# Second attention of an encoder trunk: packed 32-row score matmuls, and one written order for three engines

## The chip, the cores and the metric

One NeuronCore of a Trainium2 chip runs the whole program. The metric is device time in microseconds (us) for one execution, lower is better. Matrices are multiplied by TensorE (PE), sums, maxima and subtractions run on VectorE (DVE), exponentials and copies on ScalarE (ACT), more elementwise work on GpSimd (POOL), and SyncE (SP) issues most transfers (DMAs). SBUF is the working memory with 128 partitions (rows); matmuls write to PSUM, eight banks of 128 x 512 numbers.

## The reference

Two layers over 1024 tokens of 1024 features. The change lies in the attention of the second one (multi-head latent attention, 16 heads), whose core is:

```python
q = (rmsnorm(cq, q_norm) @ w_uq).reshape(B, S, N_HEADS_B, 64 + 32)
q_nope, q_rope = q[..., :64], q[..., 64:]
kv = (rmsnorm(ckv, kv_norm) @ w_ukv).reshape(B, S, N_HEADS_B, 64 + 64)
k_nope, v = kv[..., :64], kv[..., 64:]
q_rope, k_rope = rope(q_rope, cos, sin), rope(k_rope, cos, sin)
s = einsum(q_nope, k_nope) + einsum(q_rope, k_rope)      # k_rope is shared by the heads
p = softmax(s * scale)
o = einsum(p, v)
y = (o * silu(gate)) @ w_out
```

So a score sums 64 products of the head's own part and 32 of the rotary part.

## The kernel before, in words

Products are made accurate with a split: a number x is a rounded high part h (type float32r) and a low part l = x - h. A product a*b is then three matmuls, a_h b_h + a_h b_l + a_l b_h; `mm3` (lines 90 to 94) issues them.

The program is one instruction stream per engine, built by Python loops. `run` (line 109) puts the parts into `manual_schedule(engines=FIXED)`, where FIXED is PE and SP: those two engines issue in the order in which the Python code is written. The order of ACT, DVE and POOL is chosen by the framework's scheduler.

`layer_b_in` (line 1015) makes the latents of the second layer. `latents_t` (line 1083) transposes them, and puts the shared rotary key into rows 64 to 127 of the key tiles `kb`, high and low, with zeros between, for even and odd heads at different rows. `b_rope_rows` (line 1224) copies those rows by DMA from POOL's queue to the key tile of a later head; three pairs of key tiles serve the heads in turn. The last step of `layer_b_in` weaves the last two gate products with the first pair's `b_turn` and `b_qk` (line 1159).

`b_turn` (line 1238) makes the rotary queries for four heads: a product into PSUM, multiplications by cosines and sines on DVE, sums of 32 rows on POOL. `b_qk` (line 1265) makes the queries and keys of a pair of heads: for each half of the tokens a product for q (six matmuls) and one for k (three), whose high parts ACT copies and whose low parts DVE subtracts, head by head on 64 rows; ACT and POOL put the rotary rows beside them. `b_v` (line 1206) makes the values of four heads in four products. `b_weights` (line 1189) splits the next pair's weights, and `b_wload` (line 1175) loads those behind.

`layer_b_attention` (line 1316) sweeps 128 units u: one head and 128 queries against all 1024 keys, eight units a head, 16 a pair. For each u:

- `front` (line 1321): the scores s, two halves of 512 keys with three matmuls of 128 rows each, into one of two PSUM tiles of two banks.
- `soft` (line 1333): DVE takes the negative maximum of a row (line 1336).
- `expo` (line 1339): ACT takes the exponential with its sum (line 1344); every fourth unit DVE takes reciprocals of four sums (line 1348).
- `middle` (line 1367), for u - 2: PE transposes the eight blocks of the probabilities (line 1376) into two of four rotating PSUM banks (tag "t"); ACT copies the high part (line 1379), DVE subtracts the low part (line 1380).
- `back` (line 1384), for every two units: 16 matmuls of 256 queries give the output (line 1396) in one bank; ACT copies both halves of its rows (lines 1405, 1406), POOL adds them and multiplies by the gate (lines 1407, 1408). Every second time the reciprocal sums are transposed (line 1399) and `spread` (line 1350) sends them through DRAM to all rows; `normalise` (line 1361) multiplies them in on POOL.

Projections for later heads are Python generators, of which the loop (lines 1413 to 1454) runs one step here and there between the units. In the last pair the loop loads and splits output weights and splits the first outputs (`b_yt`, line 1465). `layer_b_out` (line 1500) does the output product and the normalisation.

PSUM in this stage: two tiles of two banks for scores, four banks for everything else. SBUF tiles of 4 KB a row come from two pools, G with 33 and H with 14.

## Time and profile before

| | us |
|---|---|
| median of 3 runs | 1358.07 |
| lowest, highest | 1356.69, 1358.98 |
| the profiled execution | 1356.85 |
| its span, first to last instruction | 1355.1 |
| first score matmul, first output matmul in it | 776.2, 1246.6 |

The span is what the profile shows; the profiled execution's own time is 1.75 us longer. A row of a group names the line of the kernel, the engine, the operation, what is written and read, the count, and behind the bar the busy time in us and the mean length of one in ns. A matmul's record lasts longer than the distance to the next one's start, because matmuls are pipelined; how long a stretch takes is read from starts. A row of waits names who waited, for whom, the total in us, the count and the longest. In a row of stretches the busy times of PE, its weight loads (PEld), DVE, ACT and POOL stand with their counts, then the granted clock of TensorE, the DMA share and GB/s. Rows of SPq are issues of DMAs.

### The profile page before, as it was taken

The page shows a single profiled execution, that of the slowest core. Times are in us where ns is not written, and L with a number is a line of the kernel's source. Part 1 is how long each engine was busy: PE and PEld are TensorE (multiplying, and loading weights), DVE is VectorE, ACT ScalarE, POOL GpSimd, SP SyncE. Part 2 cuts the span into 40 slices and gives each one's busy share as a digit, 9 for nine tenths or more (in the row PEclk, how much of TensorE's full clock was granted, in tenths as well). Part 3 has the DMA queues.
Part 4 walks back from the last instruction along what each step waited for, and adds up shares of the span by engine and source line. Part 5 has one row for each costly group of instructions (what it writes and reads, how often), then busy time and mean ns, then how long its engine had stood idle before and what let it go on. Part 6 is the DMA issues. An engine that isn't in the chain of part 4 may idle for free.

```text
span 1355.1 us, 20458 instructions
## 1 busy us (share of the span) xinstructions
PE 1328.6 (98%) x7435; PEld 1143.5 (84%) x7435; DVE 855.9 (63%) x1480; ACT 799.1 (59%) x1631; POOL 565.3 (42%) x552
## 2 busy tenths in 40 slices
PE   9999999999999999999999999999999999999997
PEld 7888888888888888888988888898889889898776
DVE  7645445445544345376733378878787788777887
ACT  4665556544444423165632397889698878887411
POOL 0333123213231477425533444734654473444861
PEclk8999999999999999999999999999999999999999
DMA  9423211113244374371163011111121111113322
GB/s 369 146 35 64 33 58 54 49 27 126 96 132 132 92 179 160 124 252 47 50 182 115 2 33 34 24 38 25 32 52 28 30 25 28 25 55 124 110 93 93
DMA packets 45117, 114.30 MB, mean 84 GB/s; under 512 B 6893, under 2 KB 13342, under 8 KB 45017
## 3 DMA queue, kind: packets, MB, share of 16 engines
q1 hardware_dynamic: 40204, 100.41, 24.0%
q0 software_dynamic: 4192, 12.27, 3.7%
q8 instruction: 59, 0.97, 0.3%
q14 instruction: 42, 0.34, 0.1%
q10 hardware_dynamic: 620, 0.31, 0.1%
HBM read 96.43 MB, written 8.67 MB: 78 GB/s over the span
## 4 chain that ended last, share of the span: by engine, by line
PE 78%; DVE 7%; ACT 7%; DMA 3%; issue 3%; SPq 0%; ACTq 0%; DVEq 0%
PE pj L92 8%; PE pj L94 8%; PE pj L93 8%; PE o L1396 6%; PE t L1376 5%; PE po L92 4%; PE po L93 4%; PE po L94 4%; PE s L92 3%; PE s L94 3%; PE s L93 3%; PE pg L92 2%; PE pg L93 2%; PE pg L94 2%; PE ip L272 2%
## 5 line engine op out<-in xcount | busy, mean ns | idle before, releaser
L92 PE MATMUL pj<-uh,wh 128*128 128x512 f32 x528 | 217.2, 411 | 0.7 <-ACT wh L104 0.7
L94 PE MATMUL pj<-uh,wl 128*128 128x512 f32 x528 | 207.0, 392 | 0.0
L93 PE MATMUL pj<-ul,wh 128*128 128x512 f32 x528 | 206.8, 392 | 0.0
L1336 DVE TENSOR_REDUCE mb<-s 128x1 f32<-128x1024 f32 x128 | 155.8, 1217 | 48.7 <-PE s L94 47.9
L1380 DVE TENSOR_TENSOR ptl<-t,pth 128x512 fp32r<-128x512 f32 x256 | 165.3, 681 | 5.2 <-ACT pth L1379 3.0
L1379 ACT CAST pth<-t 128x512 fp32r<-128x512 f32 x256 | 139.5, 590 | 37.4 <-PE t L1376 34.0
L1344 ACT ACTIVATE pr<-s,mb 128x1024 f32<-128x1024 f32 x128 | 144.2, 1126 | 15.4 <-DVE mb L1336 14.7
L105 POOL TENSOR_TENSOR wl<-wraw,wh 128x1024 fp32r<-128x1024 f32 x42 | 106.3, 2536 | 102.4 <-ACT wh L104 75.4
L1376 PEld LDWEIGHTS t<-ident,pr 128*128 128x128 f32 x1024 | 119.3, 141 | 19.1 <-DVE ptl L1380 2.8
L1376 PE MATMUL t<-ident,pr 128*128 128x128 f32 x1024 | 133.1, 273 | 2.1 <-DVE ptl L1380 2.1
L1396 PE MATMUL o<-pth,vq 128*128 128x256 f32 x512 | 130.4, 292 | 1.1 <-DVE ptl L1380 1.1
L1396 PE MATMUL o<-ptl,vq 128*128 128x256 f32 x512 | 125.6, 283 | 0.8 <-DVE ptl L1380 0.5
L564 ACT ACTIVATE sb<-sb,stat 128x256 f32<-128x256 f32 (+1 forms) x144 | 67.0, 466 | 94.8 <-DVE stat L558 94.7
L94 PEld LDWEIGHTS pj<-uh,wl 128*128 128x128 f32 x528 | 99.1, 188 | 22.2
L1407 POOL TENSOR_TENSOR osum<-osum 64x256 f32<-64x256 f32 x64 | 47.9, 748 | 163.7 <-ACT osum L1406 162.6
L92 PEld LDWEIGHTS pj<-uh,wh 128*128 128x128 f32 x528 | 99.7, 189 | 15.1 <-ACT wh L104 1.1
L93 PEld LDWEIGHTS pj<-ul,wh 128*128 128x128 f32 x528 | 99.8, 189 | 14.0
L92 PE MATMUL s<-kb,q 128*128 128x512 f32 x256 | 105.8, 413 | 0.1
L94 PE MATMUL s<-kb,q 128*128 128x512 f32 x256 | 100.4, 392 | 0.0
L93 PE MATMUL s<-kb,q 128*128 128x512 f32 x256 | 100.4, 392 | 0.0
L1396 PEld LDWEIGHTS o<-ptl,vq 128*128 128x128 f32 x512 | 97.8, 191 | 1.7 <-DVE ptl L1380 1.7
L1396 PEld LDWEIGHTS o<-pth,vq 128*128 128x128 f32 x512 | 97.6, 191 | 1.8 <-DVE ptl L1380 1.7
(289 smaller groups left out, 3128.2 us busy)
## 6 DMA issues: line engine op xcount, KB each, us to landing
wraw<-wa SPq DMA_DIRECT2D x36, 512.0 KB
ada<-ada_row SPq DMA_DIRECT2D x64, 256.0 KB
wraw<-wo_a SPq DMA_DIRECT2D x18, 512.0 KB
ada<-ada_ss SPq DMA_DIRECT2D x16, 512.0 KB
kb<-kb POOLq DMA_DIRECT2D x30, 256.0 KB, 4.5
f<-f_d SPq DMA_DIRECT2D x18, 256.0 KB
xr<-x SPq DMA_DIRECT2D x8, 512.0 KB
xn_d<-z POOLq DMA_DIRECT2D x8, 512.0 KB, 4.5
```

The source lines that it names most:

```text
L92: mm(out, wh, xh, start=start, stop=False)
L93: mm(out, wh, xl, start=False, stop=False)
L94: mm(out, wl, xh, start=False, stop=stop)
L105: (lo_engine or self.nc.gpsimd).tensor_tensor(l[:, :width], raw[:, :width], f32(h[:, :width]), op=ALU.subtract)
L564: nc.scalar.activation(sb[:, a * w : a * w + w], sb[:, a * w : a * w + w], AF.Exp, bias=stat[:, 0, hh, t : t + 1], scale=-1.0, accum_out=s ...
L1336: nc.vector.tensor_reduce(m[:, 0:1], s, axis=AX.X, op=ALU.max, negate=True)
L1344: nc.scalar.activation(pr, s, AF.Exp, bias=m[:, 0:1], accum_out=dens[u // 8][:, u % 8 : u % 8 + 1])
L1376: nc.tensor.transpose(pt[:, c * P : c * P + P], pr[:, kt * P : kt * P + P], self.ident)
L1379: nc.scalar.copy(h, src)
L1380: nc.vector.tensor_tensor(l, src, f32(h), op=ALU.subtract)
L1396: nc.tensor.matmul(po[:, 0:256], v, pts[j][x][:, c * 256 : c * 256 + 256], start=n == 0, stop=n == 15)
L1407: nc.gpsimd.tensor_tensor(w3[mine, 0:256], w3[mine, 256:512], w3[mine, 0:256], op=ALU.add)
```

## The change

The work is done in cycles w of two units (the same head, 256 queries), and three things change.

**Scores.** A score has 64 x 3 + 32 x 3 = 288 rows of products where the old form used three matmuls of 128. The new one uses two full matmuls and 32 rows of a third. In the first, queries `qa` hold the high part in rows 0 to 63 and the low part in 64 to 127, against the key's high part in both. In the second, `qb` holds the high part above and the rotary rows, high and low, below, against the key's low part and the rotary key's low and high part. What is left, high rotary query times high rotary key, has 32 rows: `small` issues it for two units and two halves of the keys as four matmuls at `tile_position` rows 0, 32, 64 and 96, from a query tile `q3` whose four row groups hold the two units' queries, and a key tile `kr` that holds the two halves of the keys. They end the sums of the first unit and begin those of the second.

**Placing.** High and low parts of q and k are now split for both heads in one instruction of 128 rows (`staged`), and SP's queue carries the 64-row pieces to their places. The rotary queries go to DRAM (`b_rope_store`) and from there to `qb` and `q3` (`b_rotary`). The rotary key rows stay in the three key tiles for all heads.

**Order.** The stage runs under ORDERED: ACT and DVE also issue as written. One cycle's order is the loop below; a cycle has the rest of a projection at one place, mostly one projection a cycle (four in the first, two in some that make values). Of the output, ACT copies one half of the rows and DVE adds the other from PSUM.

The core of the diff, where `high`, `low`, `turned`, `maximum`, `expo` and `values` hold the same instructions as `middle`, `soft`, `expo` and `back` did, for one unit a (0 or 1) of a cycle or for both:

```diff
+ORDERED = FIXED | {mybir.EngineType.Activation, mybir.EngineType.DVE}
...
-                    self.layer_b_attention()
+                    with tc.manual_schedule(engines=ORDERED):
+                        self.layer_b_attention()
...
+        self.kr = self.M.tile([P, 512], F32R, name="kr")
...
-            for e, (h, l) in enumerate(self.kb):
-                dst.append((h[64:128, c : c + P], l[64:128, c : c + P], slice(64 - 64 * e, 128 - 64 * e), 3))
...
+            for rows in ((slice(0, P),) if i < 4 else (slice(32, 64), slice(96, 128))):
+                nc.scalar.copy(self.kr[rows, sl], pt[rows, 3 * P : 4 * P])
+            nc.vector.tensor_tensor(
+                self.kb[0][1][64:96, c : c + P], pt[32:64, 3 * P : 4 * P], f32(self.kr[32:64, sl]), op=ALU.subtract
+            )
...
+                weave((first, 5184.0), (self.b_turn_first(), 2600.0))
...
-        weave((chain(gate(6, 1, self.mbank), gate(7, 1, self.mbank)), 10368.0), (chain(self.b_turn(0), self.b_qk(0)), 9000.0))
+        weave((chain(gate(6, 1, self.mbank), gate(7, 1, self.mbank)), 10368.0), (self.b_qk_first(), 4500.0))
...
-    def b_rope_rows(self, hd):
-
-        for src, dst in zip(self.kb[(hd - 2) % 3], self.kb[hd % 3]):
-            self.nc.gpsimd.dma_start(dst[64:128, :], src[64:128, :])
+    def b_rope_rows(self):
+        dma, first = self.nc.gpsimd.dma_start, self.kb[0][1]
+        for j in range(2):
+            dma(first[96:128, j * 512 : j * 512 + 512], self.kr[32 * j : 32 * j + 32, :])
+        for n in (1, 2):
+            dma(self.kb[n][1][64:128, :], first[64:128, :])
...
+    def b_rope_store(self, rd, ab, sl, engine):
         nc = self.nc
+        hl = self.ht(F32R, "rope")
+        nc.scalar.activation(hl[:, 0:512], ab[:, 0:512], AF.Copy)
+        engine.tensor_tensor(hl[:, 512:1024], ab[:, 0:512], f32(hl[:, 0:512]), op=ALU.subtract)
+        for a in range(2):
+            for x in range(2):
+                nc.sync.dma_start(rd[:, x, a, :, sl], f32(hl[64 * a : 64 * a + 64, x * 512 : x * 512 + 512]))
...
+    def b_turn(self, p, hf):
+        nc = self.nc
+        if hf == 0:
+            self.b_rope_rows_d(p)
+        sl = slice(hf * 512, hf * 512 + 512)
+        ps = self.b_product(self.wu[p], 384, sl)
+        ab = []
+        def turn():
+            t = self.ht(F32, "ab")
+            for i in range(2):
+                nc.vector.tensor_tensor(t[:, i * 512 : i * 512 + 512], ps, self.tabs[i][:, sl], op=ALU.mult)
+            if hf:
+                self.tabs = None
+            w = self.ht(F32, "absw")
+            for a in range(2):
+                nc.sync.dma_start(w[64 * a : 64 * a + 64, 0:512], t[64 - 64 * a : 128 - 64 * a, 512:1024])
+            for rows, op in ((slice(0, 64), ALU.subtract), (slice(64, 128), ALU.add)):
+                nc.gpsimd.tensor_tensor(t[rows, 0:512], t[rows, 0:512], w[rows, 0:512], op=op)
+            ab.append(t)
+        def store():
+            self.b_rope_store(self.rope_d[p], ab.pop(), sl, nc.gpsimd)
+        return turn, store
...
+    def b_rotary(self, p):
+        nc = self.nc
+        third = (self.ht if p else self.gt)(F32R, "q3")
+        rd = self.rope_d.pop(p)
+        for e, (qa, qb, k) in enumerate(self.heads):
+            rows = rd[2 * (p % 2) + e]
+            nc.sync.dma_start(f32(qb[64:128, :]), rows.rearrange("x a c t -> (x a c) t"))
+            q3 = third[:, e * 512 : e * 512 + 512]
+            for g in range(4):
+                src = rows[0].rearrange("a c (i z t) -> (a c) i z t", z=2, t=P)[:, :, g // 2, :]
+                nc.sync.dma_start(f32(q3[32 * g : 32 * g + 32, :]).rearrange("p (i t) -> p i t", t=P), src)
+            self.q[2 * p + e] = (qa, qb, q3)
+    def b_qk(self, p, kind, hf):
...
+        heads = self.heads
+        up, down = slice(0, 64), slice(64, 128)
+        if kind == "q":
+            ps = self.b_product(w, 0, sl)
+            places = [(((qa, up), (qb, up)), ((qa, down),)) for qa, qb, k in heads]
+        else:
+            ps = self.mbank()
+            ch, cl = self.lat[2]
+            self.mm3(ps, h[:, 256:384], l[:, 256:384], ch[:, sl], cl[:, sl], True, True)
+            places = [(((k[0], up), (k[0], down)), ((k[1], up),)) for qa, qb, k in heads]
+        def staged():
+            hl = self.ht(F32R, "hl")
+            nc.scalar.copy(hl[:, 0:512], ps)
+            nc.vector.tensor_tensor(hl[:, 512:1024], ps, f32(hl[:, 0:512]), op=ALU.subtract)
+            for x in range(2):
+                for e in range(2):
+                    src = f32(hl[64 * e : 64 * e + 64, x * 512 : x * 512 + 512])
+                    for t, rows in places[e][x]:
+                        nc.sync.dma_start(f32(t[rows, sl]), src)
...
+        def full(w, a):
+            hd, t = w // 4, 2 * (w % 4)
+            (qa, qb, q3), k = self.q[hd], self.kb[hd % 3]
+            ts = slice((t + a) * P, (t + a) * P + P)
+            for n, (q, kk) in enumerate(((qa, k[0]), (qb, k[1]))):
+                for j in range(2):
+                    ks = slice(j * 512, j * 512 + 512)
+                    nc.tensor.matmul(sc[w][a][:, ks], q[:, ts], kk[:, ks], start=n == a == 0, stop=n == a == 1)
+            if a and w % 4 == 3:
+                self.q.pop(hd)
+        def small(w):
+            hd, t = w // 4, w % 4
+            q3 = self.q[hd][2]
+            for g in range(4):
+                rows = slice(32 * g, 32 * g + 32)
+                ks = slice((g % 2) * 512, (g % 2) * 512 + 512)
+                nc.tensor.matmul(
+                    sc[w][g // 2][:, ks], q3[rows, t * P : t * P + P], self.kr[rows, :],
+                    start=g >= 2, stop=g < 2, tile_position=(32 * g, 0),
+                )
...
+        def output(w):
+            hd, t0 = w // 4, (w % 4) * 256
+            e, po = hd % 2, ob.pop(w)
+            mine, other = slice(64 * e, 64 * e + 64), slice(64 - 64 * e, 128 - 64 * e)
+            g = self.gT[hd // 2][mine, t0 : t0 + 256]
+            w3 = self.ht(F32, "osum")
+            nc.scalar.copy(w3[mine, 0:256], po[other, 0:256])
+            if w % 2:
+                spread(w // 2, po)
+            nc.vector.tensor_tensor(w3[mine, 256:512], po[mine, 0:256], w3[mine, 0:256], op=ALU.add)
+            nc.gpsimd.tensor_tensor(g, w3[mine, 256:512], g, op=ALU.mult)
...
+        for w in range(nw + 2):
+            p, r = divmod(w, 8)
+            now, old = w < nw, 1 <= w <= nw
+            more = p + 1 < NPAIR_B
+            if now:
+                sc[w] = [self.PB.tile([P, 1024], F32, tag="s", bufs=2, name=self.nm("s")) for _ in range(2)]
+                full(w, 0)
+                small(w)
+            if old:
+                turned(w - 1, 0)
+            if now:
+                maximum(w, 0)
+            if old:
+                high(w - 1, 0)
+                low(w - 1, 0)
+                if w % 2 == 0:
+                    reciprocal(w - 1)
+            if now:
+                expo(w, 0)
+                full(w, 1)
+                maximum(w, 1)
+            if old:
+                turned(w - 1, 1)
+                high(w - 1, 1)
+                low(w - 1, 1)
+            splits = []
+            if p % 2 == 0 and now and r < 2:
+                splits += [self.b_v(p // 2, j) for j in (range(4) if w == 0 else () if w == 1 else (2 * r, 2 * r + 1))]
+            if more and r == 3:
+                self.b_heads(p + 1)
+            if more and 3 <= r <= 6:
+                splits.append(self.b_qk(p + 1, "kqkq"[r - 3], (r - 3) // 2))
+            if more and p % 2 and r in (0, 2):
+                turn, store = self.b_turn(p + 1, r // 2)
+                splits.append(turn)
+                rot.append((w + 1, store))
+            late = splits.pop() if w >= 8 and r == 1 and p % 2 == 0 and splits else None
+            for f in splits[:2]:
+                f()
+            if now:
+                expo(w, 1)
+            for f in splits[2:]:
+                f()
+            if more and r == 6:
+                self.b_rotary(p + 1)
+            if w >= 2:
+                values(w - 2)
+                output(w - 2)
+            if late:
+                late()
+            while rot and rot[0][0] <= w:
+                rot.pop(0)[1]()
+            if w == 0:
+                self.b_weights(1)
+            if r == 7 and p + 2 < NPAIR_B:
+                self.b_weights(p + 2)
+                if p % 2 == 0:
+                    self.b_tabs()
+            if p == 7:
+                if r < 4:
+                    self.b_wo_load(r)
+                if 1 <= r <= 4:
+                    self.b_wo_split(r - 1, nc.gpsimd)
+                if r >= 5:
+                    self.b_yt(r - 5, 0)
+                if r == 7:
+                    for b in range(4, 8):
                         self.b_wo_load(b)
+            if w == nw:
+                self.b_yt(3, 0)
                 self.b_rows()
                 self.b_out_blocks(0, range(4))
+            if w == nw + 1:
                 self.b_out_blocks(1, range(4))
+            if w >= 5 and w % 2:
+                normalise((w - 5) // 2)
```

More of the change, by code (lines that the diff above doesn't have):

```diff
@@ L1133, in layer_b_in @@
                 gq[b + 2] = self.bw_load(b + 2)
-            for _ in gate(b, 0, self.bank if b < 2 else self.mbank):
-                pass
+            first = gate(b, 0, self.bank if b < 2 else self.mbank)
+            if b < 7:
+                for _ in first:
+                    pass
+            else:
+                weave((first, 5184.0), (self.b_turn_first(), 2600.0))
             if b == 0:
@@ L1147, in layer_b_in @@
                 self.kb.append([self.ht(F32R, "kb") for _ in range(2)])
-                self.b_rope_rows(2)
+                self.b_rope_rows()
             if b == 1:
@@ new lines, in staged, with direct @@
+        def staged():
[7 more added lines that the diff above has]
+                        nc.sync.dma_start(f32(t[rows, sl]), src)
+        def direct():
+            for e in range(2):
+                src = ps[64 * e : 64 * e + 64, :]
+                for t, rows in places[e][0]:
+                    nc.scalar.copy(t[rows, sl], src)
+            for e in range(2):
+                (t, rows), = places[e][1]
+                h, hr = places[e][0][0]
+                nc.vector.tensor_tensor(t[rows, sl], ps[64 * e : 64 * e + 64, :], f32(h[hr, sl]), op=ALU.subtract)
@@ L1313, in mbank, with b_qk_first @@
+        return staged if p else direct
+    def b_qk_first(self):
+        self.b_heads(0)
+        self.b_rotary(0)
+        for hf in range(2):
+            for kind, cost in (("q", 1300.0), ("k", 650.0)):
+                split = self.b_qk(0, kind, hf)
+                yield cost
+                split()
+                yield 0.0
     def mbank(self, name="m"):
@@ new lines, in turned, with part, high @@
+        def turned(w, a):
+            pr = prs.pop((w, a))
+            tb[w, a] = []
+            for j in range(2):
+                t = self.mbank("t")
+                for c in range(4):
+                    kt = 4 * j + c
+                    nc.tensor.transpose(t[:, c * P : c * P + P], pr[:, kt * P : kt * P + P], self.ident)
+                tb[w, a].append(t)
+        def part(w, a, j, x):
+            return pts[w][j][x].rearrange("p (k q) -> p k q", k=4)[:, :, a * P : a * P + P]
+        def high(w, a):
+            if a == 0:
+                pts[w] = [(self.gt(F32R, "pth"), self.gt(F32R, "ptl")) for _ in range(2)]
+            for j in range(2):
+                nc.scalar.copy(part(w, a, j, 0), tb[w, a][j].rearrange("p (k q) -> p k q", k=4))
@@ new lines, in low, with values @@
+        def low(w, a):
+            for j, t in enumerate(tb.pop((w, a))):
+                src = t.rearrange("p (k q) -> p k q", k=4)
+                nc.vector.tensor_tensor(part(w, a, j, 1), src, f32(part(w, a, j, 0)), op=ALU.subtract)
+        def values(w):
+            hd = w // 4
+            po = ob[w] = self.mbank("o")
+            x = [(kt, x) for kt in range(8) for x in range(2)]
+            for n, (kt, i) in enumerate(x):
+                v = self.vq[hd // 4][kt // 2][:, (kt % 2) * 512 + (hd % 4) * P : (kt % 2) * 512 + (hd % 4) * P + P]
+                c = (kt % 4) * 256
+                nc.tensor.matmul(po[:, 0:256], v, pts[w][kt // 4][i][:, c : c + 256], start=n == 0, stop=n == 15)
+            pts.pop(w)
+            if w % 16 == 15:
+                self.vq.pop(hd // 4)
+            if w % 2:
+                nc.tensor.transpose(po[0:4, 256:384], dens[hd][:, 2 * (w % 4) - 2 : 2 * (w % 4) + 2], self.ident)
```

248 lines of the change are left out of this document (69 added, 179 removed).

## The prediction

> **What bounds the kernel now.** I read the page's busy times first, then the busy times by stretch of the second attention, then who waited for whom in it, then TensorE's timeline over one cycle (two units of 128 queries).
>
> ```profile
> span 1355.1 us, 20458 instructions
> PE 1328.6 (98%) x7435; PEld 1143.5 (84%) x7435; DVE 855.9 (63%) x1480; ACT 799.1 (59%) x1631; POOL 565.3 (42%) x552
> ```
> ```profile
> core 0: us, PE busy (x) PEld busy (x) DVE busy (x) ACT busy (x) POOL busy (x), PEclk, DMA share, GB/s
> 911.40:972.20 60.80, 60.31 (x394) 53.63 (x393) 48.49 (x66) 48.26 (x96) 30.16 (x33) 1.00 0.13 30
> 972.20:1033.00 60.80, 59.56 (x398) 53.14 (x397) 48.68 (x68) 52.94 (x106) 31.74 (x36) 1.00 0.15 35
> ```
> ```profile
> PE m L92 <- DVE kb L1306: 3.3, 7, 0.5
> PE t L1376 <- DVE ptl L1380: 2.1, 3, 0.8
> PE o L1396 <- DVE ptl L1380: 1.1, 2, 0.8
> ```
>
> A pair of heads (eight cycles) takes 60.8 us and TensorE is busy for about 60 of them; VectorE and ScalarE for 48 to 53. TensorE's waits in the whole second attention are the three rows of the last fence, 6.5 us together. So the stage is TensorE's own instruction stream, at a full granted clock, and what counts is how much of it goes. Busy time overlaps, so lengths must be read from starts:
>
> ```profile
> 1002.99 0.40 PE L92 MATMUL s<-kb,q 128*128 128x512 f32 x1
> 1003.22 0.40 PE L93 MATMUL s<-kb,q 128*128 128x512 f32 x1
> ...
> 1004.15 0.40 PE L94 MATMUL s<-kb,q 128*128 128x512 f32 x1
> 1004.38 1.03 PE L1376 MATMUL t<-ident,pr 128*128 128x128 f32 x8
> 1005.17 0.47 PE L92 MATMUL s<-kb,q 128*128 128x512 f32 x1
> 1005.49 0.39 PE L93 MATMUL s<-kb,q 128*128 128x512 f32 x1
> ...
> 1006.64 1.04 PE L1376 MATMUL t<-ident,pr 128*128 128x128 f32 x8
> 1007.43 0.36 PE L1396 MATMUL o<-pth,vq 128*128 128x256 f32 x1
> ...
> 1009.42 0.27 PE L1399 MATMUL o<-ident,den 128*4 128x128 f32 x1
> 1009.45 0.48 PE L92 MATMUL s<-kb,q 128*128 128x512 f32 x1
> ```
>
> One cycle without a projection lasts from 1002.99 to 1009.45, 6.46 us. Six score matmuls fill 1004.38 - 1002.99 = 1.39 us, 0.232 each; eight transposes 0.79; the values 1.99. The first matmul behind transposes is followed after 0.32 instead of 0.23: changing back from a transpose costs 0.09, changing to one nothing.
>
> **The term that matters: score matmuls.** There are twelve of 512 columns a cycle now. The change keeps eight and adds one packed group of four, each on 32 rows, into four different banks. So 4 x 0.232 = 0.93 us a cycle go, and X, the length of the packed group, comes. Projections, values and transposes keep their matmuls and cancel out. No row shows a packed group. From below, X is one matmul's 0.23, if four go side by side and the change of mode is free. From above it is four in turn with a change on both sides, 0.93 + 2 x 0.09 = 1.11. The nearest rows for "fewer rows, then all rows" stand at the start, at a slow clock:
>
> ```profile
> 7.55 1.02 PE L348 MATMUL pl<-oh,rb 33*128 33x512 f32 x2
> 8.50 1.18 PE L165 MATMUL pz<-zeros 128*128 128x512 f32 x2
> 9.47 0.85 PE L220 MATMUL pm<-sc,ada 128*128 128x1 f32 x4
> ```
>
> Two matmuls on 33 rows take 0.95, the two full ones behind them 0.97: no extra is seen at that border, which speaks for the lower half, though these rows aren't placed in tiles. I take X = 0.23 for the stream, + 3 x 0.05 because each further tile needs its own weights (a transpose, a load of 128 columns and a pass of 128, takes 0.79 / 8 = 0.10, half of it the load), + 0.09 for one change back = 0.47. A cycle gains 0.93 - 0.47 = 0.46, and 64 cycles 29 us. At the ends of X it is 45 us gained or 12 us lost.
>
> The Trainium skill (TensorE: Matmul & The Clock Gate, Measured speedup vs the span model) gives 3.07 times for four K=32 row tiles at N=512. By it X would be 0.93 / 3.07 = 0.30 and the gain about 40 us; no run here shows it yet.
>
> **Can the other engines follow a cycle of 6.0 us?** ScalarE and VectorE get a written order too, so a late step holds all that is queued behind it. These are their slots:
>
> ```profile
> 1004.58 1.23 DVE L1336 TENSOR_REDUCE mb<-s 128x1 f32<-128x1024 f32 x1
> 1005.72 1.28 DVE L1380 TENSOR_TENSOR ptl<-t,pth 128x512 fp32r<-128x512 f32 x2
> 1006.92 1.22 DVE L1336 TENSOR_REDUCE mb<-s 128x1 f32<-128x1024 f32 x1
> ```
> ```profile
> 1002.18 1.12 ACT L1344 ACTIVATE pr<-s,mb 128x1024 f32<-128x1024 f32 x1
> ...
> 1003.28 0.59 ACT L1379 CAST pth<-t 128x512 fp32r<-128x512 f32 x1
> ...
> 1005.02 1.07 ACT L1379 CAST pth<-t 128x512 fp32r<-128x512 f32 x2 [0.38 <-PE t L1376]
> 1005.98 1.13 ACT L1344 ACTIVATE pr<-s,mb 128x1024 f32<-128x1024 f32 x1
> ```
>
> A maximum holds VectorE for 1.14 us, a pair of low parts 1.20; an exponential holds ScalarE 1.10, a pair of casts 0.96. Count from the first packed matmul of a cycle. TensorE: packed group to 0.47, transposes to 1.26, second unit's full rows to 2.28, transposes to 3.07, values to 5.06, next first unit's full rows to 6.0. A matmul's record is 0.39 long where the next starts after 0.23, so a result is there 0.16 behind its slot. VectorE: first maximum 0.63 to 1.8, low parts to 3.0, second maximum to 4.1, low parts to 5.3. ScalarE: casts from 1.1 to 2.1, exponential to 3.2, casts to 4.2, second exponential to 5.3. The next packed group writes the bank that this exponential reads, at 6.0: 0.7 us in hand, less what the semaphores take. The sum of the two halves of the output moves from GpSimd to VectorE:
>
> ```profile
> L1279 DVE TENSOR_TENSOR q<-m,q 64x512 fp32r<-64x512 f32 x32 | 22.0, 688 | 27.6 <-ACT q L1278 27.1
> L1405 ACT COPY osum<-o 64x256 f32<-64x256 f32 x64 | 23.5, 368 | 3.3 <-PE o L1396 1.7
> L1407 POOL TENSOR_TENSOR osum<-osum 64x256 f32<-64x256 f32 x64 | 47.9, 748 | 163.7 <-ACT osum L1406 162.6
> L1471 DVE TENSOR_TENSOR ytb<-gT,ytb 128x512 fp32r<-128x512 f32 x11 | 16.4, 1497 | 6.1 <-ACT ytb L1470 6.1
> ```
>
> Half of L1279's columns make it some 0.35 to 0.4 us, from about 5.8 (behind ScalarE's copy) to 6.2; the next maximum is due at 6.63. VectorE's 5.2 us of work in a plain cycle fit in 6.0 with 0.4 in hand. I cost the move at nothing; without that cover it is 0.4 x 64 = 26 us. ScalarE sheds a copy of 0.37. A cycle with a query projection adds 6 x 0.23 = 1.39 to TensorE and at most 0.69 to VectorE, so there the cover grows. The banks rotate by four: the second of two projections in a cycle (the values' projections) makes the probabilities' product wait from 4.5 for a low part that ends at 4.7; 0.2 us in six cycles, 1 us. A rotary step's cast stands at the end of ScalarE's next cycle, 12.7 counted from its own cycle's group: multiplies to 6.7, two swaps through SP by 8.8 (prices below), two sums on GpSimd of 1.5 (L1407's 0.75 for half as many columns) by 11.8. I cost it at nothing; were GpSimd 2 us late, ScalarE's casts and TensorE's transposes behind them would lose 1 us, six times.
>
> **Transfers.** The split halves of q and k now go through SP's queue: six pieces a projection, 24 a pair, and ten rotary pieces a pair. What they would cost is seen on SP:
>
> ```profile
> 797.91 0.27 SPq L1358 DMA_DIRECT2D den_d<-rden  x1
> 799.08 0.45 SPq L1359 DMA_DIRECT2D rden<-den_d  x1
> ```
>
> An issue of 64 rows takes 0.45 us, and a write is followed by its reader after 1.2. In the seventh cycle of a pair 6 + 10 issues stand in line, 7.2 us from about 5.3 on. The first head's eleven are out by 10.3 and landed by 11.5; the next pair's first score is due at 7.4 + 6.0 - 0.9 = 12.5. So one microsecond in hand; behind these SP holds the denominators' round trip, which GpSimd needs a cycle later. I take 2 us for all seven joints; with the cover gone it is 1 to 2 us each, up to 14. GpSimd loses the key rows' copies and half of the output's sum; busy for 30 to 32 us of a pair now, it stays far from a bound.
>
> **Ends.** Cycle 1 has no values to hide its chain: 1.5 us. The first pair's rotary rows now go through DRAM before the first score: four multiplies of 0.69, two sums and a split of up to 1.5, a cast of 0.6, four writes and the first head's five reads of 0.45, and two landings of 1.2 make 14.3 us, against the 66 matmuls of gate and projections at 0.23, 15.2, behind the last rotary product. VectorE has the projections' splits beside it: 0 to 3 us lost, I take 1. In the last pair three steps like L1471, 1.5 us each, enter VectorE's order with 0.4 in hand: 3 x 1.1 less what the next cycles return, 2. The 3.3 us at L1306 go, since that wait was for a bank whose reader is now placed ahead. With the joints and the banks, 1.5 + 1 + 2 + 2 + 1 - 3.3 = 4 us are lost.
>
> **Sum.** The profiled execution took 1356.85 us, 1.75 more than its span; 29 - 4 = 25 us less gives 1332. The median of the three runs, 1358.07, is 1.2 above the profiled one, so I put 1333.
>
> **Rivals.**
> *The array must be empty at each change.* A matmul is 0.39 long at a spacing of 0.23, so 0.16 is still in flight; if the group waits for that and the transposes wait for the group, X = 0.23 + 0.15 + 2 x 0.16 = 0.70, the gain 15 - 4 = 11 us, the time 1347. Against it: the border at L348 shows nothing. The Trainium skill (TensorEngine Tiling (Array Packing), Key Properties) says that a change of tiling mode drains TensorE, which is this rival; the trace has no change of that kind. Chance 0.15.
> *The four go in turn (the slower side).* Nothing in the trace shows two matmuls at once. If each 32-row tile streams alone, X = 1.11 and the cycle grows by 0.18: 12 + 4 us, 1374. It decides from X = 0.87 on (0.93 less 4 / 64). Chance 0.15.
> *The written order binds.* If semaphores, a slot of the shared buffers or an SP transfer eat the 0.4 to 0.7 us in hand and 0.25 more, each cycle is 6.25 and the gain 13 - 4 = 9: 1349. For it: VectorE's and ScalarE's chains are 5.3 us long without any delay. Chance 0.15, with 0.03 of it beyond 6.5 us, slower.
> *Packing is nearly free.* X = 0.23 to 0.30 and no waits added: 40 to 45 us, 1313 to 1318. Chance 0.15.
>
> **How the numbers follow.** My case, about 1324 to 1342, has 0.40. A measurement of this kernel tells about 0.2%, 2.7 us. Slower: 0.14 from the tiles in turn and 0.03 from the order; same: 0.04 from the edges of the three middle cases; faster 0.79. The range runs from the free packing, 1314, through both middle rivals to 1360, and leaves out the tiles in turn and little below.
>
> **What the new profile would show.** Packed matmuls of 32 rows whose starts lie under 0.1 us apart, and first transposes about 0.47 behind the first of them; in turn they would lie 0.23 apart. Plain cycles of 6.0 us, pairs of about 57. VectorE's second maximum with almost no idle time ahead of it. I am wrong if TensorE waits for `pr` (the written order), for q or q3 from DMA (SP's queue), or if the border of the group holds over 0.3 us.

## The result and the profile after

| | before | after |
|---|---|---|
| median, 5 runs each, us | 1358.07 | 1367.04 |
| lowest, highest | 1355.99, 1358.98 | 1362.32, 1368.15 |
| the profiled execution, its span | 1356.85, 1355.1 | 1367.04, 1365.2 |
| first score, first output matmul | 776.24, 1246.63 | 779.19, 1259.55 |
| between the two | 470.4 | 480.4 |

The changed kernel is slower by 0.6%: ratio 1.0061, interval 1.0041 to 1.0081. In the profiled executions the first score comes 3.0 us later, the stage takes 10.0 more, and what follows it takes 2.8 less.

First the head of the page of the changed kernel. Then two rows for the same pair of heads, from its first cycle (number 32) to the next pair's: the kernel before, and the changed one. Last, TensorE's waits in the whole stage.

```profile
span 1365.2 us, 20719 instructions
PE 1323.1 (97%) x7435; PEld 1112.4 (81%) x7435; DVE 862.7 (63%) x1486; ACT 747.2 (55%) x1519; POOL 439.5 (32%) x415
```
```profile
1011.71:1071.37 59.66, 59.16 (x401) 53.25 (x400) 46.80 (x65) 51.59 (x103) 26.43 (x31) 1.00 0.15 35
```
```profile
1022.12:1080.06 57.94, 57.50 (x402) 48.31 (x399) 46.85 (x69) 42.86 (x86) 11.90 (x13) 1.00 0.38 93
```
```profile
PE t L1466 <- DVE ab L1321: 8.1, 3, 2.9
PE o L1490 <- DVE ptl L1481: 6.1, 6, 1.4
PE s L1424 <- DMA q<-rope_d: 3.4, 4, 2.4
PE s L1435 <- ACT pr L1449: 1.5, 3, 0.6
```

This pair takes 57.9 us where it took 59.7, though it still holds a wait in its first cycle, so a part of the intended gain is there. The GB/s in the last column rise from 35 to 93. TensorE's waits have tripled (6.5 us before, these four rows are 19.1), and the largest group is three waits of 2.7 us for `ab` at line 1321: a bank that VectorE's product of the rotary queries and their tables still has to read.

TensorE's timeline over a cycle without a projection (start, length, engine, line):

```profile
1015.98 1.11 PE L1424 MATMUL s<-kb,q 128*128 128x512 f32 x4
1017.01 0.50 PE L1435 MATMUL s<-kr,q 32*128 32x512 f32 x4
1017.45 1.09 PE L1466 MATMUL t<-ident,pr 128*128 128x128 f32 x8
1018.29 1.17 PE L1424 MATMUL s<-kb,q 128*128 128x512 f32 x4
1019.30 1.03 PE L1466 MATMUL t<-ident,pr 128*128 128x128 f32 x8
1020.10 0.36 PE L1490 MATMUL o<-pth,vq 128*128 128x256 f32 x1
...
1022.12 0.48 PE L1424 MATMUL s<-kb,q 128*128 128x512 f32 x1
```

It lasts 6.14 us (1015.98 to 1022.12) against 6.46. The view puts the four packed matmuls into one row; taken singly, they start at 1017.014, 1017.017, 1017.021 and 1017.024, so they begin together. The packed group and its borders: first full matmuls to group 1.03 (four spacings of 0.232 are 0.93, so 0.10 extra), group to transposes 0.44, eight transposes 0.84 (0.79 before, 0.05 extra). So X is about 0.10 + 0.44 + 0.05 = 0.59, and a cycle gains 0.32, 64 cycles 20 us.

With 20 us less, the stage would last 450; it lasts 480. The lengths of its 64 cycles, compared with the same kind of cycle elsewhere in the stage, place the 30 us: cycles 9, 25 and 41 take 12.12, 12.10 and 12.42 in place of 6.14, 18.2 us; their neighbours 3.6; cycles 0 to 2 some 4.0; the first cycles of a new pair (16, 32, 48, 56) 3.0; cycles 30 and 46 1.8. In cycle 9, VectorE, then TensorE, then TensorE's clock (columns as in the fence of stretches):

```profile
848.32 0.69 DVE L1321 TENSOR_TENSOR ab<-m,tab 128x512 f32<-128x512 f32 x1 [4.81 <-DMA tab<-qtab]
850.00 0.69 DVE L1321 TENSOR_TENSOR ab<-m,tab 128x512 f32<-128x512 f32 x1 [0.98 <-DMA tab<-qtab]
```
```profile
846.87 1.18 PE L1424 MATMUL s<-kb,q 128*128 128x512 f32 x4
850.74 1.11 PE L1466 MATMUL t<-ident,pr 128*128 128x128 f32 x8 [2.69 <-DVE ab L1321]
853.18 0.44 PE L1490 MATMUL o<-pth,vq 128*128 128x256 f32 x1 [1.32 <-DVE ptl L1481]
853.41 0.41 PE L1490 MATMUL o<-ptl,vq 128*128 128x256 f32 x1
```
```profile
848.05:853.37 5.32, 1.30 (x9) 1.03 (x10) 3.97 (x6) 0.93 (x1) 0.18 (x1) 1.00 0.34 78
853.37:856.79 3.42, 3.42 (x18) 3.35 (x17) 2.68 (x4) 2.44 (x6) 3.07 (x3) 0.50 0.00 0
```

VectorE stands 4.81 + 0.98 us for the tables; in the written order the next maximum and the low parts are behind it. TensorE waits 2.69 for a bank and 1.32 for the next one, and then runs for 3.42 us at a granted clock of 0.50: a record of the values' matmuls lasts 0.41 us instead of 0.28. Of the 6 us that this cycle loses, 4.5 are the two waits (from the second unit's full rows to the transposes 3.87 instead of 1.01, from these to the values 2.44 instead of 0.80) and 1.5 the clock (the values 3.50 instead of 2.02). Why the tables come late is to be read from SyncE's issues, and from two rows of stretches beside them:

```profile
837.01 2.52 SPq L1355 DMA_DIRECT2D q<-rope_d  x4
839.63 0.47 SPq L1505 DMA_DIRECT2D den_d<-rden  x1
841.83 0.49 SPq L1506 DMA_DIRECT2D rden<-den_d  x1
842.42 0.54 SPq L1194 DMA_DIRECT2D wuraw<-wu_o  x1
843.05 2.43 SPq L1306 DMA_DIRECT2D tab<-qtab  x4
```
```profile
839.60:843.00 3.40, 3.40 (x23) 2.92 (x21) 3.17 (x6) 3.33 (x7) 1.47 (x2) 1.00 0.20 52
843.00:848.30 5.30, 5.05 (x35) 3.82 (x33) 0.51 (x1) 2.08 (x5) 1.28 (x1) 1.00 0.91 241
```

The tables (line 1306) go out at the end of a line, 1.5 us before cycle 9 begins. Two explanations compete: the line is long (some 0.6 us an issue, with six staged pieces, ten reads and three more ahead), or the tables stand behind issues that themselves wait for data. From 839.63 to 843.05 the line moves two denominators' transfers and a weight load, which take 1.5 us to issue, and for 1.65 us it stands still, until the denominators have been written and can be read back. Meanwhile the DMA engines are busy a fifth of the time; behind it they are nearly full (0.91, 241 GB/s) with the tables, a megabyte in four loads, until VectorE's first product starts at 848.32.

### The profile page after: what moved, and what is told of

Its sections match the earlier page's. It is cut to its first block, busy times and chain, and to the rows that moved or that the text cites. A ratio compares the mean times of both kernels' runs of the same rounds, so it can differ in the third digit from the quotient of the medians.

```text
span 1365.2 us, 20719 instructions
## 1 busy us (share of the span) xinstructions
PE 1323.1 (97%) x7435; PEld 1112.4 (81%) x7435; DVE 862.7 (63%) x1486; ACT 747.2 (55%) x1519; POOL 439.5 (32%) x415
## 4 chain that ended last, share of the span: by engine, by line
PE 83%; DMA 6%; DVE 5%; ACT 2%; SPq 2%; issue 1%; DVEq 0%; ACTq 0%
PE pj L93 8%; PE pj L95 8%; PE pj L94 8%; PE o L1490 7%; PE s L1424 7%; PE t L1466 7%; PE po L93 4%; PE po L95 4%; PE po L94 4%; PE ip L274 2%; PE s L1435 2%; DMA ada<-ada_row 2%; PE t L577 2%; PE pg L93 2%; PE pg L94 2%; PE pg L95 2%
## 5 line engine op out<-in xcount | busy, mean ns | idle before, releaser
L1424 PE MATMUL s<-kb,q 128*128 128x512 f32 x512 | 151.4, 417 | 3.8 <-DMA q<-rope_d 3.4
L1466 PE MATMUL t<-ident,pr 128*128 128x128 f32 x1024 | 137.6, 278 | 8.5 <-DVE ab L1321 8.1
L1466 PEld LDWEIGHTS t<-ident,pr 128*128 128x128 f32 x1024 | 115.1, 141 | 33.8 <-issue 10.0
L1490 PE MATMUL o<-ptl,vq 128*128 128x256 f32 x512 | 129.4, 289 | 0.0
L1490 PEld LDWEIGHTS o<-pth,vq 128*128 128x128 f32 x512 | 100.5, 196 | 11.0 <-DVE ptl L1481 9.6
L1424 PEld LDWEIGHTS s<-kb,q 128*128 128x128 f32 x512 | 88.3, 193 | 18.2 <-issue 5.4
L1490 PEld LDWEIGHTS o<-ptl,vq 128*128 128x128 f32 x512 | 100.9, 197 | 1.5
L1519 POOL TENSOR_TENSOR gT<-osum,gT 64x256 f32<-64x256 f32 x64 | 46.9, 732 | 164.0 <-DVE osum L1518 145.6
L105 ACT ACTIVATE wh<-wraw 128x1024 fp32r<-128x1024 f32 x54 | 57.1, 1058 | 50.7 <-DMA wraw<-wa 22.8
```

Source lines behind the costliest of these rows:

```text
L1424: nc.tensor.matmul(sc[w][a][:, ks], q[:, ts], kk[:, ks], start=n == a == 0, stop=n == a == 1)
L1466: nc.tensor.transpose(t[:, c * P : c * P + P], pr[:, kt * P : kt * P + P], self.ident)
L1490: nc.tensor.matmul(po[:, 0:256], v, pts[w][kt // 4][i][:, c : c + 256], start=n == 0, stop=n == 15)
```

## The experiments

Each median is given with its ratio to the kernel before, measured beside it (medians of 1356.5 to 1357.84), and the interval of the ratio. A cycle's length is taken from its first score matmul to the next cycle's; a plain cycle is one without a projection.

**The order and the group.** First the changed kernel with one thing undone at a time.

e_turn_later moves the first half's rotary product one unit back:

```diff
-            if more and p % 2 and r in (0, 2):
+            if more and p % 2 and r in (1, 2):
```

> The first rotary product of an odd pair is made in the pair's second cycle instead of its first; the second one stays in the third cycle. Nothing else changes. Theory A (the cosine and sine tables are asked for too late: they stand in SP's queue behind the 16 pieces of the seventh cycle, VectorE waits for them in its written order, TensorE stops and its clock is halved for some microseconds): the three cycles of 12.1 to 12.4 us fall to about 6.2 to 7.6, their neighbours to 7.6, and the whole time by about 20 us, to 1345 to 1350. Rival B (the written order itself binds: a rotary step anywhere in a cycle delays all behind it): the long cycle moves one cycle on and the time stays within 5 us of 1367.

1357.32, ratio 1.0003 [0.9987, 1.0019]: between the two theories, 7 us above the first. Cycles 9, 25 and 41 fall to 7.5, which is what a cycle with a product takes. But cycles 16, 32, 48 rise to 10.3, 11.3, 9.6, with TensorE waiting for the reads into the score rows, and cycles 13, 14, 29, 45 and 46 take 1.1 to 2.0 us more, where ScalarE stands for slots held by stores that have not landed. One row for cycle 16, two for cycles 12 and 14:

```profile
897.59 0.70 PE L1424 MATMUL s<-kb,q 128*128 128x512 f32 x2 [1.59 <-DMA q<-rope_d]
```
```profile
870.73 1.12 ACT L1449 ACTIVATE pr<-s,mb 128x1024 f32<-128x1024 f32 x1 [2.66 <-DMA rope_d<-rope]
882.89 0.37 ACT L1515 COPY osum<-o 64x256 f32<-64x256 f32 x1 [2.48 <-DMA rope_d<-rope]
```

e_free_order lets the scheduler order ScalarE and VectorE again:

```diff
-                    with tc.manual_schedule(engines=ORDERED):
+                    with tc.manual_schedule(engines=FIXED):
```

> Only the written order is undone: ScalarE and VectorE are again ordered by the framework's scheduler in the second attention; packed scores, the placing through SP's queue and TensorE's order stay. Theory A: the tables are as late as before, but VectorE need not stand in front of them if the scheduler places the multiplications later, so at best the 20 us of the three rotary cycles are saved, 1347 to 1360; if it places them as the written order does, 1367. Rival B (the written order binds in every cycle): plain cycles fall below 6.1 us too and the time falls by 25 us or more, to 1342 or less.

1373.89, 1.0118 [1.0087, 1.0149], above both theories. Plain cycles stay at 6.14 to 6.2, cycles with a key projection take 7.50 instead of 6.83, and the cycles around the tables 9 to 10.8. So the written order as a whole is not what costs: without it the kernel takes 7 us more.

e_full_rows replaces the packed group by four matmuls of 128 rows, e_one_tile puts all four on rows 0 to 31:

```diff
-                    sc[w][g // 2][:, ks], q3[rows, t * P : t * P + P], self.kr[rows, :],
-                    start=g >= 2, stop=g < 2, tile_position=(32 * g, 0),
+                    sc[w][g // 2][:, ks], q3[:, t * P : t * P + P], self.kr,       # e_full_rows
+                    start=g >= 2, stop=g < 2,
...
+                    sc[w][g // 2][:, ks], q3[0:32, t * P : t * P + P], self.kr[0:32, :],   # e_one_tile
+                    start=g >= 2, stop=g < 2, tile_position=(0, 0),
```

> The packed group becomes four matmuls on all 128 rows, each 512 columns, at the same place in the order; the scores then hold wrong sums, so this is a time only: order and placing of the changed kernel with as much score work on TensorE as before. Theory A (the group costs about 0.62 us a cycle with both changes of mode, where four full matmuls cost 0.93): plain cycles 6.45 us, the time 15 to 20 us longer, about 1385. Rival C (packing saves nothing, since the array runs empty around the group): within 5 us of 1367.

> All four matmuls of the group read rows 0 to 31, so they share one tile of the array and can't run side by side; scores hold wrong sums, a time only. If the four do run side by side in the changed kernel (theory A): the group lasts three matmuls longer, 0.7 us a cycle, 45 us in all, about 1410. If they ran in turn there (my forecast's slower rival): no change, 1367 within 5 us.

e_full_rows: 1377.93, 1.0130 [1.0105, 1.0155], plain cycles 6.46 to 6.52. e_one_tile: 1391.40, 1.0238 [1.0219, 1.0257], plain cycles 6.82 to 6.88. In a cycle of e_one_tile the way from group to transposes is 1.12 (1035.74 to 1036.86), where the changed kernel has 0.44:

```profile
1035.74 1.19 PE L1435 MATMUL s<-kr,q 32*128 32x512 f32 x4
1036.86 1.09 PE L1466 MATMUL t<-ident,pr 128*128 128x128 f32 x8
```

So on four tiles the four do run side by side. On one tile, four matmuls of 32 rows take 0.36 us a cycle more than four of 128 rows at the same place (6.82 against 6.46), though the columns are as many: that is the price of going over to 32 rows and back. Both runs lose less in all than 64 times a cycle, and less than expected, since the waits shrink as TensorE slows (cycles 9, 25 and 41 take 9.5 to 12.2 us): the waits take back part of whatever TensorE saves.

e_no_group leaves the group out (the full matmuls then begin and end their sums themselves):

```diff
-                small(w)
```

> The group of four 32-row score matmuls is left out (the scores lack the rotary part and the third product; the loads of its operands stay). Theory A: what the group costs on TensorE is its stream and two changes of the array's shape, 0.62 us a plain cycle, and no other engine is near: a plain cycle falls from 6.15 to about 5.53, the four full matmuls from 1.03-1.11 to 0.93. If the joints of the unit pairs waited for nothing else, 64 x 0.62 = 40 us would go: 1327. With the transfers as they are, the joints give back some of it: 1330 to 1345. Rival B: the written order of VectorE and ScalarE binds below 6.15, and the plain cycle stays above 5.8: 1345 or more.

1339.92, 0.988 [0.9849, 0.9911]. A cycle with a query projection falls from 7.57 to 6.98, one with a key projection from 6.83 to 6.23, the plain one behind them from 6.14 to 5.54, so X is 0.60 counted this way too. In the last pair, where plain cycles follow each other, they run at 5.58 to 6.13, mean 5.9, with ScalarE busy for 33.0 and VectorE for 30.6 of 34.9 us:

```profile
1180.90:1215.80 34.90, 34.45 (x245) 30.83 (x244) 30.59 (x45) 32.96 (x62) 17.16 (x13) 1.00 0.26 85
```

Cycles 9, 25 and 41 grow to 12.9, 13.6 and 13.3. Between theory and rival: TensorE bounds the changed kernel at 6.14, and the chain over ScalarE and VectorE is next at about 5.9.

e_two_groups tells what X is made of. It has the group twice in a row, in the version with GpSimd's queue below (median 1341.97):

```diff
                 small(w)
+                small(w, True)
```

> All rotary transfers issued by GpSimd as in the run that gave 1342, and every packed group issued twice in a row (the high rotary products then count twice in the scores). Theory B (borders): the 0.60 us that a group costs are mostly the two changes of shape, and a second group behind the first costs only its stream: from the first packed matmul to the transposes 0.43 becomes 0.65 to 0.75, a plain cycle 6.15 becomes 6.4: 64 x 0.25 = 16 us more, 1354 to 1362. Rival S (stream): four packed matmuls and their weights need 0.43 and more themselves: 0.43 becomes 0.9 or more, a plain cycle 6.6: 1368 or more.

1350.16, 0.9948 [0.9932, 0.9964]. Its timeline:

```profile
1004.71 1.09 PE L1424 MATMUL s<-kb,q 128*128 128x512 f32 x4
1005.73 0.74 PE L1435 MATMUL s<-kr,q 32*128 32x512 f32 x8
1006.40 1.09 PE L1466 MATMUL t<-ident,pr 128*128 128x128 f32 x8
```

From group to transposes 0.67 instead of 0.44: four packed matmuls more cost 0.23 to 0.24, one matmul's stream (0.232). Plain cycles are 6.37 where they were 6.14. So of X = 0.60 the stream is 0.24 and the two changes of shape 0.36, the same 0.36 as between e_one_tile and e_full_rows. The total rose by 8 us, not 15, in part because cycle 40 of the other run loses 3.4 us (below) and this one 0.4; the expected 1354 was missed by 4.

**The tables.** Next, what is issued where. In these kernels `nc.sync.dma_start` becomes `nc.gpsimd.dma_start` at some of the places: tables (line 1306), swap (1326), stores (1273), reads into the score rows (1351, 1355). e_tabs_pool moves the tables alone, e_pool_queue all four, e_pool_later all four with the edit of e_turn_later.

```diff
-                self.nc.sync.dma_start(t[64 * a : 64 * a + 64, :], self.A["qtab"][64 * i : 64 * i + 64, :])
+                self.nc.gpsimd.dma_start(t[64 * a : 64 * a + 64, :], self.A["qtab"][64 * i : 64 * i + 64, :])
...
-                nc.sync.dma_start(w[64 * a : 64 * a + 64, 0:512], t[64 - 64 * a : 128 - 64 * a, 512:1024])
+                nc.gpsimd.dma_start(w[64 * a : 64 * a + 64, 0:512], t[64 - 64 * a : 128 - 64 * a, 512:1024])
```

> The four loads of the rotary tables of every two pairs of heads are issued by GpSimd, the rest as in the changed kernel. Theory A: the tables come late in cycles 9, 25 and 41 because their issue stands at the end of SyncE's line, some 0.6 us an issue. Off that line they are there in time: cycles 9, 25, 41 fall from 12.1-12.4 to 6.2-6.8 and their neighbours lose the halved clock: 15 to 20 us less, 1347 to 1352. Rival B: the tables wait for a free slot of their pool, or for the transfers that share the DMA engines: the three cycles stay above 10 and the time above 1360.

> All transfers of the rotary path (tables, the swap of halves, stores of turned rows, reads into the score rows) are issued by GpSimd, whose units are busy a third of the time; SyncE keeps the staged pieces, the weights and the denominators. Theory A (SyncE's line is what is late at the joints): besides cycles 9, 25, 41 the waits at 16, 32, 48 and in 30, 46 get shorter too: 1338 to 1348. Rival B: GpSimd, which runs its line in order, is now late with the output multiplies that free ScalarE's and VectorE's slots: other cycles rise by 0.5 us or more each and the time is 1355 or more.

> As the run before it (rotary transfers issued by GpSimd), and the first half's rotary product of the next two pairs made one unit later (r = 1 and 2 in place of 0 and 2). Theory A: with the tables early and SyncE's line short no wait of more than a microsecond is left inside a pair: 1335 to 1346. Rival C: the second half follows one unit after the first, the slots of the turned rows are held by transfers, and ScalarE, in its written order, stands for them as it did when the product alone was moved: cycles 13 to 16, 29 to 32, 45 to 48 keep 8 us or more together each: 1350 or more.

e_tabs_pool: 1367.95, 1.0077 [1.0054, 1.0100]; my theory missed. Cycles 9, 25, 41 are 6.13 now, but 8, 24, 40 are 15.3 to 15.4. The tables go out at 832.51, ahead of the reads, and then the reads are late: the second four take 5.46 us to issue instead of 2.52, while the DMA engines are full (share 1.09, 222 GB/s from 837.00 to 842.50). That fits the rival's transfers that share the DMA engines.

```profile
833.82 2.53 SPq L1355 DMA_DIRECT2D q<-rope_d  x4
836.39 0.60 SPq L1351 DMA_DIRECT2D q<-rope_d  x1
837.03 5.46 SPq L1355 DMA_DIRECT2D q<-rope_d  x4
```

e_pool_queue: 1341.97, 0.9883 [0.9857, 0.9910], 25 us below the changed kernel and faster than before. Cycles 8, 9, 24, 25 and 41 hold no wait of note, and the stage takes 456 us instead of 480. TensorE's waits in the whole stage:

```profile
PE o L1490 <- DVE ptl L1481: 2.7, 5, 1.4
PE m L95 <- POOL wul L1208: 1.9, 1, 1.9
PE s L1424 <- ACT pr L1449: 0.7, 1, 0.7
PE s L1435 <- ACT pr L1449: 0.6, 1, 0.6
```

The one for `wul` is in cycle 40 (10.95 us, of which 3.4 are lost): GpSimd's split of weights stood behind its own issues. e_pool_later: 1340.95, 0.9878 [0.9853, 0.9902], not to be told from it; cycles 13, 29 and 45 lose 0.6 to 2.3 us each, cycle 40 none.

e_rot_pool moves only the reads to GpSimd, e_reads_tabs reads and tables.

> Only the reads into the score rows (ten issues a pair) are issued by GpSimd; tables, swaps and stores stay with SyncE. Theory A (one line): with the reads out of SyncE's line the tables are issued some 6 us earlier and cycles 9, 25, 41 fall from 12.1-12.4 to 6.2-7.5, cycles 8, 24, 40 stay below 8: 1342 to 1350. Rival B (the DMA engines are full there whoever issues, as when the tables alone went to GpSimd and cycles 8, 24, 40 rose to 15): the three cycles, or the ones before them, stay above 10: 1357 or more.

> The reads into the score rows and the tables are issued by GpSimd; swaps and stores stay with SyncE. Theory A: reads and tables are all that counted; the time is that of the run with all four kinds on GpSimd, 1338 to 1346. Rival B: the stores and swaps count as well, and the waits of ScalarE in cycles 16, 30, 32, 46, 48 come back, 0.5 to 1.5 us each: 1346 to 1352.

e_rot_pool: 1362.44, 1.0047 [1.0031, 1.0063], so theory A missed: with ten issues out of SyncE's line the tables still go out at 843.91, right behind the same weight load (843.19) and 2.9 us before cycle 9 instead of 1.5, and cycles 9, 25, 41 take 11.0, 10.2, 9.6. That speaks against the length of the line. e_reads_tabs: 1351.35, 0.9960 [0.9945, 0.9975]: those cycles are 6.12, while 16, 32 and 48 keep 9.6, 8.8 and 11.2 and cycle 0 takes 10.5 (6.0 in e_pool_queue), where the stores are on SyncE.

The test of place against length is e_tabs_first: everything stays on SyncE, only the four table loads are written earlier. e_tabs_first_pool adds GpSimd for swaps, stores and reads, e_tabs_first_st for swaps and stores.

```diff
                 values(w - 2)
+                if r == 7 and p + 2 < NPAIR_B and p % 2 == 0:
+                    self.b_tabs()
                 output(w - 2)
...
                 self.b_weights(p + 2)
-                if p % 2 == 0:
-                    self.b_tabs()
```

> As the changed kernel, all on SyncE; only the issue of the four table loads is moved up in its written line, from behind the denominators' two transfers and the next weights' load to right behind the reads into the score rows. Theory P (place: SyncE runs its line in order, and the two denominators' transfers and the weights' load each stand for their own data): the tables go out some 3.4 us earlier (839.6 in place of 843.05 in the first case), TensorE's wait of 2.9 us and the halved clock behind it go, cycles 9, 25, 41 fall from 12.1-12.4 to 6.2-7.5: 1345 to 1352. Rival L (length: the ten reads of 0.6 us an issue ahead of them, or the transfers themselves, are what is late): one of the cycles 8 and 9 (24 and 25, 40 and 41) stays above 9: 1357 or more.

> Tables moved up in SyncE's line, and swaps, stores and reads issued by GpSimd. Theory P: with both, no table is late, and GpSimd's line is 2 us shorter ahead of the split of the next weights than in the run that gave 1342, so the wait of 3.4 us in cycle 40 goes too: 1335 to 1341. Rival L: the tables share the DMA engines with the reads and one is late again: 1345 or more.

> Tables moved up in SyncE's line; swaps and stores issued by GpSimd, the reads by SyncE. Theory P: cycles 9, 25, 41 at 6.2-7.5, and without the stores in SyncE's line the waits at 16, 30, 32, 46, 48 stay below 1 us each: 1338 to 1346. Rival L: the reads, which both have on SyncE, are what holds the staged pieces and the first scores of the next pair: 16, 32 and 48 keep 1 us or more: 1346 to 1352.

e_tabs_first: 1351.54, 0.9959 [0.9946, 0.9972], 15.5 us below the changed kernel. SyncE's line:

```profile
838.86 2.56 SPq L1355 DMA_DIRECT2D q<-rope_d  x4
841.51 2.46 SPq L1306 DMA_DIRECT2D tab<-qtab  x4
844.07 0.42 SPq L1505 DMA_DIRECT2D den_d<-rden  x1
848.49 0.46 SPq L1506 DMA_DIRECT2D rden<-den_d  x1
849.03 0.54 SPq L1194 DMA_DIRECT2D wuraw<-wu_o  x1
```

The tables go out 5.6 us before cycle 9 (847.12) instead of 1.5. The six pieces and ten reads are still ahead of them; only the three issues are now behind them, where the reading back of the denominators stands 3.9 us for its data. Cycles 9, 25, 41 take 6.60, 7.27, 7.19, and TensorE's wait for `ab` is gone from its list. Cycle 8 rises from 8.11 to 9.03, so a little of the cost moved there; cycles 8 to 10, 24 to 26 and 40 to 42 together lose 6 us where they lost 22. The place is the cause, not the length: an issue that waits for its data holds all that is written behind it.

e_tabs_first_pool: 1342.76, 0.9890 [0.9866, 0.9914], as e_pool_queue; cycles 8, 32 and 40 (10.33, 9.18, 11.85) now wait for reads, so the expected 1335 to 1341 was missed by little. e_tabs_first_st: 1352.58, 0.9965 [0.9950, 0.9981], no better than the tables' place alone. A new wait took the gain: cycles 10, 26 and 42 take 9.2 to 10.4 us (7.7 to 8.2 in e_tabs_first), since GpSimd issues the swap behind a multiply that had waited 9.42 us for the denominators:

```profile
844.94 1.29 POOL L1525 TENSOR_TENSOR gT<-gT,rden 64x512 f32<-64x512 f32 x1 [9.42 <-DMA rden<-den_d]
846.17 1.12 POOL L1326 DMA_DIRECT2D absw<-ab  x2
```

**What the group is worth with the line clear.** e_pool_full is e_pool_queue with the group as in e_full_rows; e_pool_early is e_pool_queue with the first pair's rotary product one gate block earlier (`if b != 6` in place of `if b < 7`).

> All rotary transfers issued by GpSimd as in the run that gave 1342, and the packed group of four 32-row matmuls made into four matmuls of all 128 rows (the scores are then other sums). Theory A: with the transfers out of the way the group's gain shows in full: plain cycles rise from 6.15 to 6.46, 64 x 0.31 = 20 us more, 1358 to 1364. Rival B: at a 6.15 us cycle something else than TensorE already takes part of the gain, and less than 12 us are lost: 1354 or less.

> All rotary transfers issued by GpSimd, and the first pair's rotary product woven into the gate block before the one that it stands in now. Theory A: the first scores then wait for no read of the turned rows: first score 1.5 to 3 us earlier, 1337 to 1341. Rival B: the read waits for something else (a slot, or the copies of the first keys that the trace names next): no difference, 1341 to 1344.

e_pool_full: 1356.02, 0.9995 [0.9983, 1.0006]. Plain cycles are 6.46 to 6.52, so each loses 0.32 to 0.34, and the median loses 14 us, not 20: e_pool_queue has its 3.4 us in cycle 40, and 1.5 in cycle 63, that this run doesn't have. So with nothing late, packing is the difference between the time before and 1342: without it this version is as fast as the kernel before. e_pool_early: 1349.45, 0.9951 [0.9932, 0.9970], a miss: the first score comes at 790.5 instead of 781.6, behind waits of 4.9 and 3.1 us for the split gate weights. Why these come late stays open.

## Why the prediction was wrong

- **The term that matters, X = 0.47.** Mis-sized. It is 0.60: the stream is 0.24 (I had 0.23 + 0.15 for later weights; the four start 0.003 us apart and need no such stagger), the changes of shape 0.36 (I had 0.09). The forecast "transposes about 0.47 behind the first" came out at 0.44 by luck, as the two errors cancel there. The rival of an array empty at each change had the borders nearly right (0.32); what happens inside the array no run shows, only what the two borders cost. The gain is 20 us instead of 29. The row at line 348 (33 rows, then 128) that I held against this rival was no guide, as those matmuls aren't placed in tiles. The Trainium skill (TensorEngine Tiling (Array Packing), Key Properties) says that a change of mode drains TensorE, and the 0.36 us fit that. From the 3.07 times that the Trainium skill (TensorE: Matmul & The Clock Gate, Measured speedup vs the span model) gives for four tiles I had the estimate X = 0.30. Between full matmuls the runs show 0.93 / 0.60 = 1.55 times.
- **Transfers, "2 us for all seven joints".** This is the step that failed, with the rotary step "costed at nothing". I counted the issues ahead of the next score's operands, at 0.45 each (the staged pieces' median is 0.59), and left out the table loads altogether: they are not among the 24 pieces and ten rotary pieces, and the rotary step takes the tables as being there. They are written last in that line, behind the denominators' round trip, which stands for its own data, and a weight load. I even named the round trip, as standing behind the reads, and asked only who needs it. The cycles at the tables lose 18 us and their neighbours 3.6; moving the four issues alone (e_tabs_first) brought 15.5 of these 22 back.
- **Can the other engines follow.** Right for a plain cycle: 6.14 us without waits, and with TensorE faster ScalarE and VectorE bind at about 5.9. Wrong in its warning: a late step does hold the whole engine in a written order, but it was a transfer that was late, not GpSimd's sums.
- **Ends, 4 us lost with the joints.** The forecast had 1.5 + 1 for the start; cycles 0 to 2 lost 4.0 against e_pool_queue, and the first score came 3.0 us later. The start shifts from run to run (777.7 to 781.6 in most of these kernels), so the 3.0 is only partly the change's. The first cycles of the pairs and cycles 30 and 46, where TensorE waits for reads and ScalarE for stores, lost 4.8 us, where I had 2. The 3.3 us at the banks did go.
- **The sum.** Against the forecast of 25 us less, 10 more: 9 from X, 18 and 4 from the tables and behind them, the rest of the 35 from start and joints. The rival "the written order binds" named the SP transfer but spread it over all cycles at 0.25 us; it was six microseconds in three of them.

## What to carry to other kernels

When transfers are added to a queue that issues as written, follow every issue in that line to what it waits for: one that stands for its own data holds all behind it, and four table loads moved ahead of three issues, one of which so stands, were worth 15 us here. An issue that is moved to another engine's line stands behind that engine's waits instead (e_tabs_first_st). Put several packed groups behind each other if it can be done: side by side four matmuls cost one stream, but the way in and out cost 0.36 us a visit here, half of the 0.69 that packing saved.

## What the runs showed of the hardware

- Four 32-row matmuls of 512 columns on four tiles start 0.003 us apart and take 0.24 us together, and in turn on one tile 0.68 more than that (1.12 instead of 0.44 from the group to the transposes). A pair of changes, to 32 rows and back to 128, costs 0.36: once as 0.60 for a group less 0.24 for a second one, once as 6.82 less 6.46 in e_one_tile and e_full_rows.
- After waits of 2.69 and 1.32 us, with 1.1 us of transposes between them at full clock, TensorE's granted clock was 0.50 for 3.4 us. In e_pool_queue one wait of 1.86 us was followed by 3.4 us at 0.50 (1070.20 to 1073.60); in e_tabs_first_st one of 2.57 us was followed by a clock of 1.00 (972.20 to 979.00). So the length of a wait alone doesn't decide here. The Trainium skill (TensorE: Matmul & The Clock Gate, What's actually happening) gives an idle window of about 3.4 us for the drop; the wait of 1.86 us was shorter.
- The Trainium skill (DMA: Bandwidth & Descriptors, Issuing engines are not separate DMA queues) says that issuing on more engines saves only the time of issuing. The rate hardly changed here either (99 GB/s over the stage in the changed kernel, 104 in e_pool_queue), but 25 us went. As 15.5 us went in e_tabs_first with every issue left on SyncE, most of that is not time of issuing but the waits that held what was written behind them.
